# Head 0's gate work moved ahead of the samples' projection, and the samples' state updates moved behind their products

## The chip, the cores and the metric

One core of one Trainium2 chip runs the kernel. The metric is the device time of one execution in microseconds (us); the time before is the median of three runs. The engines are named as in the profile: PE (matrix products), DVE (vector), ACT (scalar, activations and copies), POOL (elementwise work and 16-bit splits), SP (its queue issues most DMAs).

## The reference

One inference step of a two-layer decoder: a gated linear attention (GLA) layer, then a differential-attention layer, each followed by a squared-ReLU MLP, all with a layer norm behind the residual. The model width is 1024. There are 1024 prompt tokens in one sequence, 16 learned tokens ahead of them, and 8 running samples of one token each, which carry a GLA state and a paged cache of 4096 positions. What the change touches is the GLA layer:

```python
q, k, v, r, g_low = split(x @ w_in)            # 4 heads, q and k 128 wide, v and r 256 wide
lg = log_sigmoid(g_low @ w_gate + b_gate) / 16 # a decay for every token and key element
# per head: S_t = diag(exp(lg_t)) S_{t-1} + k_t^T v_t ;  o_t = q_t S_t
b = cumsum(lg);  scores_ij = sum_d q_id k_jd exp(b_id - b_jd), j <= i
o = q exp(b) S + scores v ;  S' = exp(b_last) S + (k exp(b_last - b))^T v
out = (rms_norm(o) * silu(r)) @ w_out
```

The samples do the same with one token each from a loaded state of 4 heads x 128 x 256 (0.5 MB a sample), and write the updated state back. Everything is float32.

## The kernel before, in words

The prompt's work and the samples' work lie side by side in one program. A scheduler fixes, before anything runs, one order of instructions for each engine; on the chip each engine takes its own list in that order and waits at an instruction until its inputs and buffers are ready. So an instruction that waits holds everything behind it on its engine.

**Prompt.** The 1024 tokens lie transposed in two halves of 512 (c = 0, 1), split into a high and a low part (XH, XL). A product in float32 is three matmuls (`mm3`, L206 to L208: high x high, high x low, low x high). Weights come as 256 KB pieces through a raw buffer (L191), ACT casts the high part (L193), POOL makes the low part (L194). `proj(h)` (L304 to L332) is a generator: it makes q and k of head h (4 pieces of 24 matmuls, 512 wide), then v (4 pieces of 48 matmuls, 256 wide), which go into the wide buffer Y. The head loop (L633 to L712) runs for each of 4 heads: the gate (L640, `log_gate` L390 to L395), a running sum (`scan`, L648), seven levels of decays (`level`, L427 to L433, with block products L658 and L673 and masked copies L667), the transposes of k (L693), and the advance of the state over 8 tiles (L701 to L705), whose outputs go back into Y (L708, L709), with a norm on POOL at the end of a head (L712). Behind the loop comes the projection of r, whose Silu is kept in a tile of the same pool as the samples' weights.

**Samples.** The 32 rows (16 learned tokens, 8 samples) go through the same weights in plain float32, from 1 MB tiles (`swt`, a pool of two buffers): the projection (L354 to L366), the gates and the learned tokens' state SM (L400 to L458), the learned tokens' own scores sA (L461 to L473), then a loop over the 8 samples (L482 to L494). For each sample it loads the state into one of three slots of Y (L487), loads the sample's v row broadcast over the partitions (L488, `vs`, into one half of a `swt` tile), multiplies state by q on PE into one accumulator (L490), multiplies the v row by k on POOL (L491), updates the state with four DVE instructions (L493) and writes it out (L494). Behind it come the output's norm (`so`, L508; `soT`, L515 and L516), the product with w_out (`s_rows`, L520 to L526), the residual norm (`s_post`, `s_ln`, L529 to L570), the MLP (L578 to L588, with 16 tiles of w1 and 16 of w2) and the projection of the second layer (L594 to L599 and once more `s_rows`; 12 tiles).

In the program's text the whole of the samples' work stands ahead of the head loop; only 8 of head 0's projection pieces are put into it by hand (`next(first)`). The order on the engines mixes the two.

Of the kernel before, what the change touches and what calls it, by code (L numbers as in the profile page):

```python
# [11 lines left out]
F32 = mybir.dt.float32  # L12
# [9 lines left out]
P = 128  # L22
D = 1024
# [91 lines left out]
def hybrid_step(ctx, tc, A, dbg=None, upto=9):  # L115
# [158 lines left out]
    dma(graw, wir[:, :, 3072:3088])  # L274
    for c in range(2):
# [65 lines left out]
    for c in range(2):  # L341
# [6 lines left out]
        V.tensor_tensor(go, go, ga, op=ALU.add)  # L348
    qk = {}
    first = proj(0, qk)  # L350
    next(first)
# [3 lines left out]
    for k in range(NB):  # L355
# [3 lines left out]
        if k % 2:  # L359
            next(first)  # L360
    for k in range(0, NB, 2):
# [21 lines left out]
    wg = gp.tile([48, 512], F32, name="wg")  # L383
    for c in range(2):
        dma(wg[32 * c : 32 * c + 16, :], A["gla_w_gate"][0])

    def log_gate(z, n, h):

        a = t2()[:, :n]
        S.activation(a, z, AF.Abs, bias=bg[:, h : h + 1])  # L390
        S.activation(a, a, AF.Exp, scale=-1.0)
        S.activation(a, a, AF.Ln, bias=1.0)
        m = t2()[:, :n]
        V.tensor_scalar(m, z, bg[:, h : h + 1], 0.0, ALU.add, ALU.min)
        V.tensor_tensor(m, m, a, op=ALU.subtract)  # L395
        return m

# [24 lines left out]
    def level(b, q, k, u, s, eng):  # L422

        sh = [P, b.shape[1] // (2 * s), 2 * s]
        bv = b.rearrange("p (n s) -> p n s", s=2 * s)
        uv = u.rearrange("p (n s) -> p n s", s=2 * s)
        V.tensor_tensor(uv, bv, bv[:, :, s - 1 : s].broadcast_to(sh), op=ALU.subtract)  # L427
        S.activation(uv[:, :, :s], uv[:, :, :s], AF.Exp, scale=-1.0 / 16)
        S.activation(uv[:, :, s:], uv[:, :, s:], AF.Exp, scale=1.0 / 16)
        kv = k.rearrange("p (n s) -> p n s", s=2 * s)  # L430
        qv = q.rearrange("p (n s) -> p n s", s=2 * s)
        eng.tensor_tensor(uv[:, :, :s], uv[:, :, :s], kv[:, :, :s], op=ALU.mult)
        eng.tensor_tensor(uv[:, :, s:], uv[:, :, s:], qv[:, :, s:], op=ALU.mult)  # L433


# [18 lines left out]


# [26 lines left out]
    vbs = swt()  # L482
    for b in range(NS):
        stt = Y[:, 5120 + 1024 * (b % 3) : 6144 + 1024 * (b % 3)].rearrange("p (h e) -> p h e", e=256)
        vb = vbs[:, b % 2, :].rearrange("p (h e) -> p h e", e=256)
        with tc.issue_after(w_in):
            dma(stt, A["state_gla"][0, b].rearrange("h d e -> d h e"))  # L487
# [145 lines left out]
    for h in range(GH):  # L633
        if h:
            for _ in proj(h, qk):
                pass
# [1002 lines left out]
```

## Time and profile before

| | |
|---|---|
| median of three runs | 2850.98 us |
| lowest, highest | 2846.44, 2857.75 us |
| the profiled execution's own time | 2854.69 us |
| its span in the trace | 2852.8 us |
| mean granted TensorE clock | 0.986 |
| PE, DVE, ACT, POOL busy | 2741.8, 1962.4, 1095.6, 1104.5 us |

A row of the profile names the line of the program, the engine, the operation, what it writes and reads with the shape, and behind the brackets how long the engine had stood idle and which instruction or DMA released it. In a table by stage, "PE busy (x)" is the busy time and the number of instructions, and "PEclk" is the clock that the throttle granted, as a share of full speed. The part of the program that the change touches lies between about 40 and 430 us of the span; the second layer and both prompt MLPs lie behind.

### The profile page before, as it was taken

What the parts mean: (1) busy time and instruction counts of PE and PEld (TensorE: products, weight loads), DVE (VectorE), ACT (ScalarE), POOL (GpSimd) and SP (SyncE); (2) the same over time, 40 slices, a digit from 0 to 9 for tenths busy, and PEclk for the clock granted to TensorE, in tenths of its full rate; (3) what the DMA queues carried; (4) which work ended last, traced back from release to release, by engine and by line L of the source; (5) the groups of instructions that cost most, each with busy time, mean ns of one, the idle gap of its engine ahead of it and who ended that gap; (6) DMA issues with size and microseconds to landing.
All of it is one profiled execution on the core that took longest, in us unless ns stands there. A gap on an engine that the chain in (4) does not pass through costs nothing.

```text
span 2852.8 us, 52251 instructions
## 1 busy us (share of the span) xinstructions
PE 2741.8 (96%) x19849; PEld 2247.6 (79%) x19849; DVE 1962.4 (69%) x3045; ACT 1095.6 (38%) x2230; POOL 1104.5 (39%) x744
## 2 busy tenths in 40 slices
PE   8889999999999999999999999899999999999997
PEld 5676677997777777777798989677898889797985
DVE  2565454658887887677667740887648878878788
ACT  3233344242221321221242112777535546355553
POOL 1221212233443443444333322200026767667764
PEclk9899999999999999999999999999999999999999
DMA  7557751634798898979748995222144555555584
GB/s 246 181 178 259 262 177 33 238 105 150 259 344 306 313 352 297 362 288 327 256 158 302 366 365 173 61 62 70 38 120 88 116 128 117 132 119 115 130 190 87
DMA packets 270968, 561.23 MB, mean 197 GB/s; under 512 B 23462, under 2 KB 138732, under 8 KB 266620
## 3 DMA queue, kind: packets, MB, share of 16 engines
q1 hardware_dynamic: 251420, 521.18, 52.9%
q0 software_dynamic: 19296, 36.71, 7.9%
q8 instruction: 156, 2.56, 0.4%
q14 instruction: 96, 0.79, 0.1%
HBM read 531.42 MB, written 29.52 MB: 197 GB/s over the span
## 4 chain that ended last, share of the span: by engine, by line
PE 72%; DVE 10%; DMA 7%; issue 4%; ACT 4%; POOL 2%; SPq 0%; DVEq 0%; POOLq 0%; ACTq 0%
PE mmt L206 17%; PE mmt L207 17%; PE mmt L208 17%; PE smt L852 4%; PE axt L206 3%; PE axt L207 3%; PE axt L208 3%; PE smt L1223 2%; ACT as L1201 1%; DMA swt<-in_mlp_w 1%; PE prt L1197 1%; DVE Y L1555 1%; DVE RX L1459 1%; DMA rw<-in_mlp_w 1%; DMA pg<-in_cache_k 1%
## 5 line engine op out<-in xcount | busy, mean ns | idle before, releaser
L194 POOL TENSOR_TENSOR wlo<-raw,whi 128x512 fp32r<-128x512 f32 x256 | 371.8, 1466 | 737.4 <-ACT whi L193 656.5
L206 PE MATMUL mmt<-whi,XH 128*128 128x256 f32 (+1 forms) x1760 | 524.5, 300 | 4.2 <-ACT Y L330 3.0
L207 PE MATMUL mmt<-wlo,XH 128*128 128x256 f32 (+1 forms) x1760 | 524.5, 299 | 1.3 <-POOL wlo L194 1.3
L206 PE MATMUL mmt<-XH,whi 128*128 128x512 f32 (+1 forms) x1216 | 436.9, 360 | 6.9 <-DVE Y L922 3.0
L208 PE MATMUL mmt<-whi,XL 128*128 128x256 f32 x1536 | 434.4, 286 | 0.0
L208 PE MATMUL mmt<-XH,wlo 128*128 128x512 f32 (+1 forms) x1216 | 432.6, 356 | 0.0
L193 ACT CAST whi<-raw 128x512 fp32r<-128x512 f32 x256 | 152.8, 619 | 570.6 <-PE mmt L208 186.6
L206 PEld LDWEIGHTS mmt<-whi,XH 128*128 128x128 f32 x1760 | 332.2, 189 | 27.6 <-issue 10.6
L812 DVE TENSOR_REDUCE sc<-pg 128x16 f32<-128x1024 f32 x256 | 308.3, 1212 | 65.9 <-POOL pg L811 63.4
L207 PEld LDWEIGHTS mmt<-wlo,XH 128*128 128x128 f32 x1760 | 333.6, 190 | 24.9 <-issue 12.6
L811 DVE TENSOR_TENSOR pg<-pg,qb 128x1024 f32<-128x1024 f32 x192 | 266.3, 1394 | 59.4 <-DMA pg<-in_cache_k 51.7
L207 PE MATMUL mmt<-XL,whi 128*128 128x512 f32 x768 | 306.4, 399 | 0.0
L208 PEld LDWEIGHTS mmt<-whi,XL 128*128 128x128 f32 x1536 | 289.6, 190 | 5.5 <-issue 4.6
L206 PEld LDWEIGHTS mmt<-XH,whi 128*128 128x128 f32 x1216 | 230.3, 190 | 54.2 <-issue 12.9
L811 POOL TENSOR_TENSOR pg<-pg,qb 128x1024 f32<-128x1024 f32 x64 | 161.3, 2522 | 259.1 <-DMA pg<-in_cache_k 187.6
L208 PEld LDWEIGHTS mmt<-XH,wlo 128*128 128x128 f32 x1216 | 230.4, 190 | 34.6 <-issue 2.1
L206 PE MATMUL mmt<-whi,HH 128*128 128x512 f32 x512 | 204.8, 401 | 4.1 <-DVE Y L1036 3.7
L208 PE MATMUL mmt<-whi,HL 128*128 128x512 f32 x512 | 204.0, 398 | 0.0
L207 PE MATMUL mmt<-wlo,HH 128*128 128x512 f32 x512 | 203.5, 397 | 0.0
L1484 POOL TENSOR_TENSOR wlo<-RW,whi 128x512 fp32r<-128x512 f32 x96 | 169.7, 1807 | 55.7 <-ACT whi L1483 55.7
L1484 POOL TENSOR_TENSOR wlo<-rw,whi 128x512 fp32r<-128x512 f32 x92 | 154.2, 1727 | 80.5 <-ACT whi L1483 78.7
L207 PEld LDWEIGHTS mmt<-XL,whi 128*128 128x128 f32 x768 | 145.2, 189 | 38.2 <-issue 7.1
(424 smaller groups left out, 5716.3 us busy)
## 6 DMA issues: line engine op xcount, KB each, us to landing
pg<-in_cache_k SPq DMA_DIRECT2D x256, 512.0 KB
pg<-in_cache_v SPq DMA_DIRECT2D x256, 512.0 KB
raw<-in_mlp_w SPq DMA_DIRECT2D x164, 256.0 KB
swt<-in_mlp_w SPq DMA_DIRECT2D x32, 1024.0 KB
rw<-in_mlp_w SPq DMA_DIRECT2D x116, 256.0 KB
RW<-in_mlp_w POOLq DMA_DIRECT2D x96, 256.0 KB, 5.7
raw<-in_gla_w_in SPq DMA_DIRECT2D x48, 256.0 KB
swt<-in_gla_w_in SPq DMA_DIRECT2D x12, 1024.0 KB
```

Source lines behind the costliest of these rows:

```text
L193: S.copy(hi[:, c], raw)
L194: G.tensor_tensor(lo[:, c], raw, hi[:, c].bitcast(F32), op=ALU.subtract)
L206: TE.matmul(ps, ah, bh, start=first, stop=False)
L207: TE.matmul(ps, ah, bl, start=False, stop=False)
L208: return TE.matmul(ps, al, bh, start=False, stop=last)
L811: eng.tensor_tensor(pg, pg, qb, op=ALU.mult)
L812: return V.tensor_reduce(sc[:, n, :], pg.rearrange("p (h d) -> p h d", d=64), op=ALU.add, axis=AX.X).ins
L852: m = TE.matmul(acc[i * TS : i * TS + 16, :256], w[r, n, :], pg[r, i * 256 : (i + 1) * 256], start=n == 0, stop=n == NPG).ins
L1197: TE.matmul(pss[m], qs[i][r, ts_], ks[j][r, x:y], start=i + j == 0, stop=i == 1)
L1201: S.activation(sc_[:, m, :W], sc_[:, m, :W], AF.Exp, bias=mns[:, m : m + 1], scale=-1.0, accum_out=l[:, m : m + 1])
L1223: TE.matmul(out, at, v, start=j == 0, stop=j == t + 1)
L1484: G.tensor_tensor(lo[:, k, :], t, hi[:, k, :].bitcast(F32), op=ALU.subtract)
```

## The change

1. `wg` is loaded earlier. The functions `rstd_of`, `log_gate` and `level` are moved ahead, and the body of the head loop is split into `gate_in`, `decays`, `advance` and `head_end`; for heads 1 to 3 they are called as the body was.
2. For head 0, two pieces of the projection (q and k of half 0) are made, then the decays of half 0 (`early(0)`), all in the text ahead of the samples' projection; `early(1)` stands inside it behind its fourth tile. Their results qh and kt are kept in Y[2048:4096].
3. Head 0's `advance` and `head_end` stand right behind SM.
4. The samples' states have five slots, three in Y (5120 and up, as before) and two in a new tile `st2`. The loop over the samples only loads a state and makes its four products. The updates are a function of their own, `state_updates`, which the text calls behind the product with w_out and its norm. It takes samples 5, 6, 7, 3, 4 from the slots in which they lie and loads 0, 1 and 2 a second time (three more loads of 0.5 MB).
5. The broadcast v row lies in Y[4096:5120] and Y[5120:6144] by turns, no longer in a `swt` tile. Y[4096:5120] holds the samples' own v (`sv`) before; Y[5120:6144] is slot 0, so the v row of the second update can be loaded only when the first update's state (slot 0) has been written out.

```diff
+    first = proj(0, qk)
+    for _ in range(2):
+        next(first)
+    early(0)                      # decays(0, 0, gate_in(0, 0), (Y[...2048], ...))
     pa, pb = smt(), smt()
...
         if k % 2:
             next(first)
+        if k == 3:
+            early(1)
...
+    st = SM[:, 0, :]
+    for c in range(2):
+        st = advance(0, c, st, *parts[c])
+    head_end(0, st)
+
...
-    vbs = swt()
+    st2 = spool.tile([P, 2, 1024], F32, name="st2")
+    def slot(i):
+        t = Y[:, 5120 + 1024 * i : 6144 + 1024 * i] if i < 3 else st2[:, i - 3, :]
+        return t.rearrange("p (h e) -> p h e", e=256)
...
     for b in range(NS):
+        state_in(b, b % 5)
         for h in range(GH):
-            TE.matmul(po[...], qmk[:, h, b, :], stt[:, h, :], start=False, stop=b == NS - 1)
-        G.tensor_tensor(vb, vb, bc(skT[:, :, NM + b], [P, GH, 256], 2), op=ALU.mult)
-        for h in range(GH):
-            V.scalar_tensor_tensor(stt[:, h, :], stt[:, h, :], ses[:, h, b : b + 1], vb[:, h, :], ALU.mult, ALU.add)
-        dma(A["gla_state_s"][0, b].rearrange("h d e -> d h e"), stt)
+            TE.matmul(po[...], qmk[:, h, b, :], slot(b % 5)[:, h, :], start=False, stop=b == NS - 1)
+
+    def state_updates():
+        for n, (b, i) in enumerate(((5, 0), (6, 1), (7, 2), (3, 3), (4, 4), (0, 3), (1, 4), (2, 3))):
+            stt = slot(i)
+            if b < 3:
+                state_in(b, i)
+            vb = Y[:, 4096 + 1024 * (n % 2) : 5120 + 1024 * (n % 2)].rearrange("p (h e) -> p h e", e=256)
+            dma(vb.rearrange("p h e -> p (h e)"), A["vs"][b : b + 1, :].broadcast_to([P, D]))
+            G.tensor_tensor(vb, vb, bc(skT[:, :, NM + b], [P, GH, 256], 2), op=ALU.mult)
+            for h in range(GH):
+                V.scalar_tensor_tensor(stt[:, h, :], stt[:, h, :], ses[:, h, b : b + 1], vb[:, h, :], ALU.mult, ALU.add)
+            dma(A["gla_state_s"][0, b].rearrange("h d e -> d h e"), stt)
...
     s_post(s_rows(soT, A["gla_w_out"][0], NB), 0, spool)
+    state_updates()
...
-    for h in range(GH):
-        if h:
-            for _ in proj(h, qk):
-                pass
+    for h in range(1, GH):
+        for _ in proj(h, qk):
+            pass
```

**What stands where, DVE at the samples' output.** Line numbers of the changed kernel differ: its state update is L618, its `so` L626, its `soT` L634, its head state `gS` L462. DVE before, around the copy of the output `so`:

```order
L667 COPY_PREDICATED gAd<-masks,axt 128x128 x2
L681 COPY At_114<-gAd 32x4x32 x4
L493 SCALAR_TENSOR_TENSOR Y<-Y,ses,swt 128x256 x8
L394 TENSOR_SCALAR t_1682<-axt,bg 128x512
L395 TENSOR_TENSOR t_1682<-t_1682,t_1678 128x512
L493 SCALAR_TENSOR_TENSOR Y<-Y,ses,swt 128x256 x4
L648 SCALAR_TENSOR_TENSOR gb<-ones,t_1682 128x128 x4
L705 SCALAR_TENSOR_TENSOR gS<-SM,geb,axt 128x256
L508 COPY so<-smt 128x256
...
L493 SCALAR_TENSOR_TENSOR Y<-Y,ses,swt 128x256 x4
L499 TENSOR_SCALAR rstd<-ssq 128x1
```

Behind these stand the last four updates and the rest of the output's norm. DVE in the changed kernel, at the same copy:

```order
L462 SCALAR_TENSOR_TENSOR gS<-gS,geb,axt 128x256 x3
L618 SCALAR_TENSOR_TENSOR Y<-Y,ses 128x256 x4
L462 SCALAR_TENSOR_TENSOR gS<-gS,geb,axt 128x256
L626 COPY so<-smt 128x256
L356 TENSOR_SCALAR rstd<-ssq 128x1
L629 SCALAR_TENSOR_TENSOR so<-so,rstd,sr 128x256
L462 SCALAR_TENSOR_TENSOR gS<-gS,geb,axt 128x256
L356 TENSOR_SCALAR rstd<-gss 128x8
L618 SCALAR_TENSOR_TENSOR Y<-Y,ses 128x256
L634 COPY soT<-smt 128x2x4x32
L618 SCALAR_TENSOR_TENSOR Y<-Y,ses 128x256 x7
L618 SCALAR_TENSOR_TENSOR st_1399<-st_1399,ses,Y 128x256 x4
```

Before, 28 of the 32 update instructions stand ahead of `so` and the last four directly behind it. Now four (the first sample's) stand ahead of `so`, one (of the second sample) between `so` and `soT`, and eleven between `soT` and the gate of head 1 (the row `t_2270<-axt,bg`, a few rows on). The other sixteen stand further behind.

**The same place on SP**, which issues the loads. Before, the states, the v rows and the states' outputs in turn, with one tile of w_out ahead of most of them and three behind:

```order
L487 DMA Y<-in_state_gla 128x4x256 x3
L488 DMA swt<-vs 128x1024 x2
L240 DMA swt<-in_gla_w_out 128x2x1024
...
L494 DMA out_gla_state_s<-Y 128x4x256
L488 DMA swt<-vs 128x1024
L487 DMA Y<-in_state_gla 128x4x256 x2
L494 DMA out_gla_state_s<-Y 128x4x256
L488 DMA swt<-vs 128x1024
...
L494 DMA out_gla_state_s<-Y 128x4x256
L240 DMA swt<-in_gla_w_out 128x2x1024
L191 DMA raw<-in_gla_w_in 128x2x256
L240 DMA swt<-in_gla_w_out 128x2x1024 x2
```

In the changed kernel two tiles of w_out are issued ahead of these rows, the other two among the first updates' v rows and outputs:

```order
L615 DMA Y<-vs 128x1024
L601 DMA Y<-in_state_gla 128x4x256 x3
L619 DMA out_gla_state_s<-Y 128x4x256
L615 DMA Y<-vs 128x1024 x2
L470 DMA out_gla_state_p<-gS 128x256
L619 DMA out_gla_state_s<-Y 128x4x256
L615 DMA Y<-vs 128x1024
L619 DMA out_gla_state_s<-Y 128x4x256
L240 DMA swt<-in_gla_w_out 128x2x1024
L615 DMA Y<-vs 128x1024
L240 DMA swt<-in_gla_w_out 128x2x1024
L619 DMA out_gla_state_s<-st_1399 128x4x256
```

Each v row (L615) waits on SP until its place in Y is free, and each output (L619) until its update is done. The third and fourth tiles of w_out now stand behind such rows.

**PE at the samples' projection of the second layer**, head 3 of the prompt beside it. Before, between two tiles (L526), pieces of the projection of r stand (L206 to L208 into `mmt`) as well as the head's own block products (L658):

```order
L658 MATMUL axt<-t_3981 32x32 x7
L526 MATMUL smt<-swt,sx 32x512 x4
L658 MATMUL axt<-t_3981 32x32 x9
L658 MATMUL axt<-t_4005 32x32 x16
L526 MATMUL smt<-swt,sx 32x512 x4
L206 MATMUL mmt<-XH_86,whi 128x512
L207 MATMUL mmt<-XL_89,whi 128x512
L208 MATMUL mmt<-XH_86,wlo 128x512
L206 MATMUL mmt<-XH_87,whi 128x512
L207 MATMUL mmt<-XL_89,whi 128x512
L208 MATMUL mmt<-XH_87,wlo 128x512
```

In the changed kernel (tiles: L718 for q and k, L644 for v) only the head's block products (L410, L425) and its advance (L458 to L460) stand between the tiles:

```order
L410 MATMUL axt<-gq,gk 32x32 x16
L718 MATMUL smt<-swt,sx 32x512 x4
L459 MATMUL axt<-gS,t_4104 128x256
L460 MATMUL axt<-Y,t_4116 128x256
L425 MATMUL axt<-t_4183 32x64 x8
L425 MATMUL axt<-t_4199 32x32 x8
L644 MATMUL smt<-swt,sx 32x512 x4
L410 MATMUL axt<-t_4216 32x32 x16
L644 MATMUL smt<-swt,sx 32x512 x4
L410 MATMUL axt<-t_4240 32x32 x16
L410 MATMUL axt<-t_4264 32x32 x16
```

The projection of r begins ahead of these rows, among the first tiles, and goes on behind the third L644 tile. In both kernels a piece of r is emptied from its PSUM bank (a pool of three) by its Silu, which writes into a tile of the pool `swt`, behind all tiles of the samples' weights.

More of the change, by code (lines that the diff above doesn't have):

```diff
@@ L274, in hybrid_step @@
     dma(graw, wir[:, :, 3072:3088])
+    wg = gp.tile([48, 512], F32, name="wg")
+    for c in range(2):
+        dma(wg[32 * c : 32 * c + 16, :], A["gla_w_gate"][0])
     for c in range(2):
@@ L715, in hybrid_step @@
+            st = advance(h, c, st, *decays(h, c, pgs[c]))
+        head_end(h, st)
     fmv = Y.rearrange("p (h c m t) -> p h c m t", h=GH, c=2, m=2)
```

218 lines of the change are left out of this document (112 added, 106 removed).

## The prediction

> **What bounds the kernel now.** The first view is the page's list of busy times: PE works in 96% of the span, and none of the other engines comes near.
>
> ```profile
> span 2852.8 us, 52251 instructions
> PE 2741.8 (96%) x19849; PEld 2247.6 (79%) x19849; DVE 1962.4 (69%) x3045; ACT 1095.6 (38%) x2230; POOL 1104.5 (39%) x744
> ```
>
> The change leaves PE's matmuls as they are, so it can win only time in which PE stands idle or runs at a lower clock. The table by stage, over the part that the change touches, says where that is (the first pair of numbers is PE's, PEclk is the granted clock):
>
> ```profile
> 40.00:110.00 70.00, 70.00 (x508) 52.95 (x509) 9.52 (x27) 14.97 (x35) 15.35 (x11) 1.00 0.68 228
> 110.00:190.00 80.00, 58.89 (x751) 43.99 (x753) 60.78 (x137) 29.43 (x81) 19.45 (x11) 0.81 0.59 191
> 214.00:373.00 159.00, 149.12 (x1750) 107.80 (x1742) 87.17 (x189) 60.53 (x160) 30.25 (x17) 0.99 0.69 237
> 373.00:422.00 49.00, 45.91 (x453) 30.65 (x451) 21.11 (x43) 21.13 (x48) 11.19 (x6) 1.00 0.69 242
> 422.00:640.00 218.00, 215.58 (x1609) 192.27 (x1608) 119.29 (x194) 88.14 (x157) 65.21 (x44) 1.00 0.36 121
> ```
>
> From 110 to 190 us, where head 0's gate work and the samples' states meet, PE is idle for 80 - 58.89 = 21.1 us, and its 58.89 us ran at a clock of 0.81, which loses 0.19 x 58.89 = 11.2 us. That is **32.3 us of loss**, and the pool from which the change can draw. 40 to 110 has none, 214 to 373 has 9.9 us (the samples' MLP weights), 373 to 422 has 3.1 us (the samples' last projection).
>
> The timeline of PE names the waits inside that stage, and the chain of waits the states' loop:
>
> ```profile
> 127.40 1.49 PE L673 MATMUL axt<-t 128*32 128x64 f32 x32 [5.65 <-DVE t L433]
> 135.02 1.08 PE L490 MATMUL smt<-Y,s 128*32 128x256 f32 x8 [2.86 <-DMA Y<-in_state_gla]
> 151.60 0.64 PE L490 MATMUL smt<-Y,s 128*32 128x256 f32 x8 [3.16 <-DMA Y<-in_state_gla]
> 167.59 0.58 PE L206 MATMUL mmt<-whi,XH 128*128 128x256 f32 x1 [3.02 <-ACT Y L330]
> ```
>
> ```profile
> 140.72 5.71 DMA out_gla_state_s<-Y
> 146.44 0.37 SPq L487
> 146.91 0.46 SPq L494
> 147.46 6.64 DMA swt<-vs
> 154.29 1.88 POOL swt L491
> 156.19 3.71 DVE Y L493 x4
> 178.83 4.97 DMA swt<-in_gla_w_out
> ```
>
> PE waits for head 0's levels on DVE (5.65 us), for states whose slot must first be updated and written out (2.86, 3.16), and for a cast queued on ACT behind the level work (3.02). The change takes away the first two by what it does: the gate work gets a place under the projection, and the products no longer stand behind the updates of three slots.
>
> **The change part by part.** The stage's 32.3 us go, and in their place come these losses.
>
> (a) *Head 0's decays between projection pieces.* They issue about 60 DVE instructions a half. DVE is empty there, and PE is busy throughout:
>
> ```profile
> 40.00:90.00 50.00, 50.00 (x359) 37.42 (x359) 0.00 (x0) 8.57 (x15) 6.38 (x5) 1.00 0.81 275
> 120.41 3.10 DVE L427 TENSOR_TENSOR t<-gb 128x512 f32<-128x512 f32 x5
> 212.34 2.42 DVE L648 TENSOR_TENSOR_SCAN gb<-ones,t 128x128 f32<-128x128 f32 x4
> ```
>
> A level costs DVE 3.10 / 5 = 0.62 us for its subtraction and about as much for its two products, so seven levels with the scan (2.42) are near 12 us, and with ACT's turns between some 20 us. PE has 50 us of projection there, so it is hidden, unless PE's queue holds a block product ahead of a projection piece before DVE has got there. I take 1.5 us, between 0 and 9 (DVE's chain met in full twice is the 5.65 of the row above, and again half of it). If the cover failed wholly it would cost those 9 us.
>
> (b) *ACT's casts.* Evictions of v (the 3.02 us) still stand behind casts and exponentials on ACT. I take 2 us, 0 to 4.
>
> (c) *soT behind the second update.* The changed order puts one update instruction of the second sample in front of soT on DVE, and its v row's place is the first sample's slot. So soT, and behind it w_out's matmuls on PE, wait for a chain: the first update, its output DMA, the v row's load, POOL's multiply, the update. The chain's own rows above give 5.71 + 0.9 (two issues) + 6.64 + 1.88 = 15.1 us, and the first update itself is 1.67:
>
> ```profile
> 123.43 1.67 DVE L493 SCALAR_TENSOR_TENSOR Y<-Y,ses,swt 128x256 f32<-128x256 f32 x4
> 80.00:84.00 4.00, 4.00 (x36) 4.00 (x35) 0.00 (x0) 0.00 (x0) 0.00 (x0) 1.00 0.91 328
> 147.35 0.59 PE L702 MATMUL axt<-SM,t 128*128 128x256 f32 x2
> ```
>
> That is 16.8 us from the product of sample 5 to the row ahead of soT. Between that product and w_out PE has 69 matmuls of 256 columns at 4.00 / 36 = 0.111 us (7.7 us), three products at 0.64 (1.9; L490's row) and six matmuls of the advance's and transposes' kind at some 0.35 (2.1; from 0.59 for an overlapping pair): 11.7 us. PE is idle for about 5.1 us. Behind an idle time of this kind the clock falls, as the stage shows around the wait that ended at 167.59:
>
> ```profile
> 166.00:169.00 3.00, 1.41 (x6) 1.41 (x7) 3.00 (x10) 1.54 (x4) 1.55 (x1) 0.65 0.47 159
> 169.00:172.00 3.00, 3.00 (x15) 2.94 (x14) 2.19 (x4) 0.76 (x3) 1.91 (x2) 0.50 1.01 284
> ```
>
> 0.35 x 1.41 + 0.50 x 3.00 = 2.0 us lost by the clock. I take 7 us, between 4 (the transfers a quarter shorter) and 12 (they collide with w_out's tiles, 4.97 each). The Trainium skill, "TensorE: Matmul & The Clock Gate", section "Part 1: The HAM clock gate", has the clock halved after an idle window of about 3.4 us and given back after about 3.4 us of work: by it the clock's part would be an estimated 1.7 us, and the sum 0.3 us lower. The trace differs in that 3.02 us of idle time were enough.
>
> (d) *w_out's third and fourth tile* now stand on SP behind the first updates' outputs and v rows, where SP waits for the updates. Behind SP's waits hang only these tiles, and PE's w_out for them. I take 2 us, between 0 and 5 (a tile's 4.97).
>
> (e) *The first norm beside updates on DVE.* Seven and four update instructions stand between soT and head 1's gate, at 1.67 for four. What of them meets the norm's short DVE steps delays w1's first product: 2 us, 0 to 5 (11 x 0.42 = 4.6). Three more loads of 0.5 MB ride on SP in this stage; they and the remaining sixteen updates have the MLP's 159 us, in which DVE is idle for 72: nothing. If that cover is gone, the four rows of an update come to stand in the path of head 1's levels, 1.67 each (rival C).
>
> (f) *The MLP's weights*, 214 to 373: as now, 9.9 us.
>
> (g) *The last projection of the samples.* Its twelve 1 MB tiles have two buffers. Now PE has pieces of the projection of r between them and is the slower side. In the changed order only three pieces of r can precede (their Silu needs a `swt` buffer), so less work lies between the tiles. From the second tile to the twelfth PE has 38 matmuls of 512 columns, ten tiles, eleven sets of block products and some 14 advance matmuls:
>
> ```profile
> 101.00:110.00 9.00, 9.00 (x40) 7.33 (x40) 3.99 (x19) 3.25 (x14) 1.93 (x2) 1.00 0.23 59
> 415.06 1.06 PE L526 MATMUL smt<-swt,sx 128*32 128x512 f32 x8 [1.59 <-DMA swt<-in_diff_w_in]
> 131.50 0.66 PE L658 MATMUL axt<-t 128*32 128x32 f32 x32 [1.32 <-DVE gAd L667]
> ```
>
> 38 x 9.00 / 40 = 8.6, ten at 1.06 = 10.6, eleven at 0.66 = 7.3, 14 at 0.35 = 4.9: 31 us. The ten tiles and about four raw pieces of 256 KB are 11.5 MB, and where DMA set the pace it moved 275 GB/s (40 to 90): 42 us. So PE is idle for 11 us, where it has 3.1 now: **+8 us**. At 242 GB/s (the same place now) the tiles take 47.5, +13; at 328 (80 to 84) 35, +1.
>
> Sum: 1.5 + 2 + 7 + 2 + 2 = 14.5 us in place of 32.3, and 8 given back at the tail: a gain of 32.3 - 14.5 - 8 = 9.8 us. The profiled execution took 2854.69 us (its span 2852.8 and what lies around it), so this one would take 2844.9. It stood 3.7 us above the median of the runs; the median I forecast is **2841 us**. 0.5% is 14 us, about what a measurement of this kernel can tell from no change: 2837 and 2865 are the bounds.
>
> **The rivals.**
>
> A, *the whole pool is won.* (c) falls to 4, (d) and (e) to 0, (a) and (b) to 1 and 0, and the tail gives back 2, since a tile may run at 328 GB/s. Gain 32.3 - 5 - 2 = 25 us: 2854.69 - 25 - 3.7 = 2826. For it speaks that each wait named above is removed by the order itself; against it, the new chain in (c), each link of which has its row.
>
> B, *the tail becomes the bound, and the kernel is slower.* Two tiles that do not overlap take what the last two of now took, one behind the other:
>
> ```profile
> 407.83 7.19 DMA swt<-in_diff_w_in
> 415.08 5.48 DMA swt<-in_diff_w_in
> ```
>
> A pair in 12.7 us is 63.5 us for ten tiles; against 31 us of work PE is idle for 32, +29 over now, and with the clock at 0.50 (169 to 172) over some 12 us of the work another 6. The gain turns into 32.3 - 14.5 - 35 = -17: 2868. It decides against the change once the tail gives back over 17.8 us, and beyond 0.5% from 32 on. Against it: from 373 to 422 the same twelve tiles, PE-paced, came in 49 us.
>
> C, *POOL slows DVE's updates and levels.* The update with a POOL row beside it took 3.71 us where it takes 1.67 alone, and now eight v-row multiplies and eight updates lie beside head 1's levels:
>
> ```profile
> 156.11 2.71 POOL L194 TENSOR_TENSOR wlo<-raw,whi 128x512 fp32r<-128x512 f32 x2
> ```
>
> Four updates at 2 us more are 8 us on the path of head 1's gate: gain 2, 2849. The Trainium skill, "GPSIMD Engine Reference", section "1. Specifications", says that GpSimd's SBUF interfaces are shared with VectorE, in contention with DVE instructions of two SBUF inputs; the trace agrees in this one row.
>
> Also possible is that the change does not do what its words say: 16 of 32 updates still stand ahead of head 1's gate on DVE, five ahead of soT. That is (c) and (e), in the forecast.
>
> **How the numbers follow.** Forecast 0.40, A 0.38, B 0.12, C 0.10. The forecast's own range, by its terms' bounds taken two at a time, is 2833 to 2852. To hold the time 8 times in 10 the range takes in A with its spread and C: 2820 to 2862, and leaves out most of B. Faster by over 0.5%: A, and the lucky end of the forecast, less A's weak end: 0.40. Slower: B and a little of C: 0.14. Same: 0.46.
>
> **What would show it.** In the profile of the changed kernel: PE with no idle time of over 2 us between 40 and 110 (a); the waits of PE for states and for head 0's levels gone; one wait of 4 to 8 us ahead of w_out, released by soT on DVE, and in the chain the output DMA, a v row and POOL's multiply before it (c); waits of PE for `in_diff_w_in` of about 11 us together at the samples' last projection (g); and from there on a table as now (215.58 busy of 218). I am wrong if the idle time ahead of w_out is over 12 us, if the tail loses under 2 or over 18, or if PE loses over 10 us in head 0's decays.

## The result, and the profile after

The changed kernel takes **2834.48 us** (median of 8 runs, 2827.53 to 2839.16) against 2847.49 us for the kernel before (8 runs, 2846.10 to 2857.75): a ratio of 0.9948, 95% interval [0.9936, 0.9960]. That is 13.0 us less; the forecast was 9.8 less. A second comparison, among the experiments below, gave 0.9957 [0.9942, 0.9972].

The two profiled executions stand 24 us apart in their spans (2852.8 and 2828.8), more than the medians. A mark that both programs share tells how much of it belongs to the change: the first addition of the prompt's first MLP on DVE. These are its rows, of before and then of the changed kernel (shortest, median and longest duration in ns, then the first and last start):

```profile
L1036 DVE TENSOR_TENSOR Y<-Y,mmt x128: 634/678/692, 672.4 to 1447.1; 128x512 f32<-128x512 f32 x128
```

```profile
L1081 DVE TENSOR_TENSOR Y<-Y,mmt x128: 632/678/689, 655.8 to 1429.7; 128x512 f32<-128x512 f32 x128
```

The changed kernel is 16.6 us ahead there and 17.4 at the last of these rows. The other 7 us came up further on, where the programs do the same; single executions of one kernel differ by that much (before: 2846 to 2858).

The table by stage of the changed kernel, over the stretches of the prediction (its 110 to 214 covers two of them):

```profile
0.00:40.00 40.00, 27.79 (x128) 18.22 (x129) 16.74 (x35) 16.20 (x28) 9.69 (x12) 0.91 0.75 249
40.00:110.00 70.00, 69.84 (x888) 52.16 (x887) 35.71 (x85) 28.29 (x66) 8.81 (x7) 1.00 0.58 200
110.00:214.00 104.00, 98.64 (x782) 76.03 (x781) 55.37 (x129) 32.12 (x95) 36.19 (x20) 0.95 0.58 189
214.00:373.00 159.00, 152.52 (x1645) 110.68 (x1644) 77.26 (x177) 61.23 (x161) 36.83 (x21) 0.99 0.72 247
373.00:422.00 49.00, 40.88 (x601) 25.91 (x600) 33.13 (x84) 21.89 (x59) 1.61 (x1) 0.97 0.67 232
422.00:640.00 218.00, 216.94 (x1385) 193.96 (x1383) 110.40 (x159) 76.51 (x130) 67.81 (x46) 1.00 0.40 129
```

And the first stretch of before, which the prediction did not show:

```profile
0.00:40.00 40.00, 29.76 (x141) 20.07 (x145) 16.65 (x35) 15.95 (x28) 9.16 (x11) 0.96 0.76 252
```

PE's loss is its idle time and what the clock took from its busy time. From 110 to 214 it was 32.3 us and is 104 - 98.64 + 0.05 x 98.64 = 10.3. From 40 to 110, where DVE now has 85 instructions in place of 27, it is still nothing: the gate work is hidden whole. At the end of the samples' path (373 to 422) it rose from 3.1 to 8.1 + 0.03 x 40.88 = 9.3. PE's remaining waits, from its timeline:

```profile
182.29 1.94 PE L644 MATMUL smt<-swt,soT 128*32 128x512 f32 x8 [3.77 <-DMA swt<-in_gla_w_out]
206.31 0.41 PE L669 MATMUL smt<-ss,c_inv 128*128 128x32 f32 x2 [1.59 <-DVE ss L667]
410.20 1.06 PE L644 MATMUL smt<-swt,sx 128*32 128x512 f32 x8 [2.37 <-DMA swt<-in_diff_w_in]
415.88 0.79 PE L206 MATMUL mmt<-XH,whi 128*128 128x512 f32 x1 [1.53 <-ACT swt L774]
```

The waits for head 0's levels, for states and for ACT's cast are gone. One wait of size is new, 3.77 us at w_out; it is released by the third weight tile, not by soT. The chain that the prediction feared ahead of soT (the first update, its output DMA, a v row into the slot that it leaves, POOL's multiply, the update row) isn't what held soT. These rows of DVE, SP, POOL and PE show what ran:

```profile
157.64 1.67 DVE L618 SCALAR_TENSOR_TENSOR Y<-Y,ses 128x256 f32<-128x256 f32 x4 [1.26 <-PE smt L606]
...
167.09 0.48 DVE L618 SCALAR_TENSOR_TENSOR Y<-Y,ses 128x256 f32<-128x256 f32 x1
167.49 0.42 DVE L634 COPY soT<-smt 128x256 f32<-128x256 f32 x1
```

```profile
159.34 0.38 SPq L619 DMA_DIRECT2D out_gla_state_s<-Y  x1
159.82 0.45 SPq L615 DMA_DIRECT2D Y<-vs  x1
163.57 0.33 SPq L615 DMA_DIRECT2D Y<-vs  x1
...
172.78 0.61 SPq L240 DMA_DIRECT2D swt<-in_gla_w_out  x1
```

```profile
165.15 1.91 POOL L616 TENSOR_TENSOR Y<-Y,sqk 128x1024 f32<-128x1024 f32 x1 [2.66 <-DMA Y<-vs]
168.03 2.03 POOL L616 TENSOR_TENSOR Y<-Y,sqk 128x1024 f32<-128x1024 f32 x1 [0.98 <-DMA Y<-vs]
```

```profile
156.92 0.64 PE L606 MATMUL smt<-Y,s 128*32 128x256 f32 x8
...
169.31 1.92 PE L644 MATMUL smt<-swt,soT 128*32 128x512 f32 x16
```

Two v rows were issued here. SP waited 3.2 us for the output DMA before the second of them (163.57), and not before the first (159.82). By the semaphores of the trace the first landed at 165.02 and the second at 167.97; POOL's multiply at 165.15 and the DVE row at 167.09 waited for the first. The same semaphores tie that DVE row to the state that was loaded third, sample 7. So the row ahead of soT belongs to sample 7, the third in the text, whose v row lies in Y[4096:5120] and needs only that the first update is done. The v row that goes into slot 0, behind the output, is sample 6's, and its update stands behind soT.

From the first update to sample 7's row it took 167.09 - 157.64 = 9.45 us, and PE had work from the end of sample 5's product (156.92 + 0.64) to w_out at 169.31, 11.8 us, without a gap.

### The profile page after: what moved, and what is told of

Read it like the earlier page. It is cut to its first block, busy times and chain, and to the rows that moved or that the text cites. A ratio compares the mean times of both kernels' runs of the same rounds, so it can differ in the third digit from the quotient of the medians.

```text
span 2828.8 us, 52247 instructions
## 1 busy us (share of the span) xinstructions
PE 2735.8 (97%) x19849; PEld 2242.1 (79%) x19849; DVE 1937.3 (68%) x3045; ACT 1084.4 (38%) x2221; POOL 1115.2 (39%) x744
## 5 line engine op out<-in xcount | busy, mean ns | idle before, releaser
L194 POOL TENSOR_TENSOR wlo<-raw,whi 128x512 fp32r<-128x512 f32 x256 | 379.1, 1495 | 727.2 <-ACT whi L193 589.2
L206 PE MATMUL mmt<-whi,XH 128*128 128x256 f32 (+1 forms) x1760 | 523.1, 300 | 1.3 <-DVE ast L1244 0.9
L206 PE MATMUL mmt<-XH,whi 128*128 128x512 f32 (+1 forms) x1216 | 435.3, 359 | 6.8 <-DVE Y L967 3.0
L208 PE MATMUL mmt<-whi,XL 128*128 128x256 f32 x1536 | 433.1, 285 | 0.0
L208 PE MATMUL mmt<-XH,wlo 128*128 128x512 f32 (+1 forms) x1216 | 432.5, 356 | 0.0
L207 PEld LDWEIGHTS mmt<-wlo,XH 128*128 128x128 f32 x1760 | 332.5, 189 | 24.8 <-issue 11.8
L206 PEld LDWEIGHTS mmt<-whi,XH 128*128 128x128 f32 x1760 | 330.8, 189 | 24.6 <-issue 11.8
L208 PEld LDWEIGHTS mmt<-whi,XL 128*128 128x128 f32 x1536 | 288.8, 189 | 6.5 <-issue 5.8
L206 PEld LDWEIGHTS mmt<-XH,whi 128*128 128x128 f32 x1216 | 230.0, 189 | 49.4 <-issue 7.6
L208 PEld LDWEIGHTS mmt<-XH,wlo 128*128 128x128 f32 x1216 | 230.0, 189 | 36.6 <-issue 4.1
L206 PE MATMUL mmt<-whi,HH 128*128 128x512 f32 x512 | 204.7, 401 | 3.9 <-DVE Y L1081 3.6
L208 PE MATMUL mmt<-whi,HL 128*128 128x512 f32 x512 | 203.9, 398 | 0.0
```

What stands on the lines that cost most here:

```text
L194: G.tensor_tensor(lo[:, c], raw, hi[:, c].bitcast(F32), op=ALU.subtract)
L206: TE.matmul(ps, ah, bh, start=first, stop=False)
L207: TE.matmul(ps, ah, bl, start=False, stop=False)
L208: return TE.matmul(ps, al, bh, start=False, stop=last)
```

## The experiments

Each kernel was timed in five rounds beside the kernel before. The table gathers them. The loss of PE is taken from each kernel's table by stage: the stretch less PE's busy time times its granted clock, added over the rows of the stretch.

| kernel | ratio to before [95%] | loss 110-220 | 220-380 | 380-520 | first w1 product | last tile's product |
|---|---|---|---|---|---|---|
| before | 1 | 32.7 | 11.4 | 4.6 | 213.8 | 421.1 |
| changed | 0.9948 [0.9936, 0.9960] | 10.3 | 8.0 | 9.7 | 218.2 | 423.3 |
| changed, again | 0.9957 [0.9942, 0.9972] | 10.4 | 10.6 | 9.1 | 219.9 | 426.3 |
| early gate alone | 1.0048 [1.0029, 1.0066] | 8.6 | 8.4 | 33.0 | 245.1 | 454.4 |
| states alone | 1.0008 [0.9998, 1.0019] | 21.3 | 13.4 | 6.0 | 191.2 | 398.1 |
| early gate, Silu's own buffer | 0.9975 [0.9962, 0.9989] | 8.6 | 4.7 | 10.5 | 240.8 | 451.3 |
| changed, Silu's own buffer | 0.9925 [0.9912, 0.9938] | 10.3 | 10.0 | 4.0 | 218.9 | 429.8 |
| changed, updates behind w_out | 0.9986 [0.9975, 0.9998] | 13.0 | 9.7 | 15.4 | 225.6 | 442.8 |
| changed, updates in the MLP | 0.9991 [0.9974, 1.0009] | 3.7 | 32.6 | 9.9 | 212.3 | 444.1 |
| the same, Silu's own buffer | 0.9983 [0.9969, 0.9997] | 1.9 | 28.4 | 9.9 | 210.7 | 451.0 |
| changed, no updates | 0.9904 [0.9890, 0.9917] | 2.7 | 8.7 | 4.8 | 210.2 | 409.0 |
| before, three weight buffers | 1.0005 [0.9992, 1.0018] | 32.0 | 7.8 | 5.6 | 198.3 | 365.9 |
| changed, three weight buffers | 0.9924 [0.9908, 0.9939] | 7.4 | 8.2 | 0.3 | 230.2 | 390.1 |
| the same, Silu's own tiles | 0.9934 [0.9921, 0.9947] | 11.0 | 7.1 | 2.0 | 229.7 | 391.8 |

One profiled execution stands behind each row of losses, and it can lie well off its kernel's median: 9 us under it for the early gate with the Silu's own buffer, 9 us over it for the updates in the MLP. So the losses say where the time goes, and the ratio how much it is. Differences from the changed kernel are taken below from 0.9948; from its second ratio, 0.9957, a gain would be 2.6 us larger.

### Either half alone

My theory was that the early gate and the split states each win a part. The first kernel keeps the early gate and takes back the loop of before:

```diff
-        state_in(b, b % 5)
+        with tc.issue_after(w_in):
+            dma(stt, A["state_gla"][0, b].rearrange("h d e -> d h e"))
+        dma(vb.rearrange("p h e -> p (h e)"), A["vs"][b : b + 1, :].broadcast_to([P, D]))
         for h in range(GH):
             TE.matmul(...)
+        G.tensor_tensor(vb, vb, ...)
+        for h in range(GH):
+            V.scalar_tensor_tensor(stt[:, h, :], ...)
+        dma(A["gla_state_s"][0, b].rearrange("h d e -> d h e"), stt)
...
-    state_updates()
```

> Only the first half of the change: head 0's gate work and advance stand early, but the samples' states are loaded, multiplied, updated and written in one loop with three slots, as before. My theory: both halves of the change share the gain, since in the profile of before PE waited 7.2 us for states and 5.65 + 1.3 us for head 0's levels, and the lost clock (11.2 us) belongs to both. Then this kernel keeps the waits for states and gains about half of the change: 5 to 9 us under before, and PE waits of 5 us or more for in_state_gla are in its profile. The rival: the gate's place is all that counts, and states that wait for their slot are hidden once DVE is free of head 0's levels. Then it is as fast as the changed kernel, 12 to 15 us under before, and the waits for in_state_gla are under 2 us.

It was **slower** than before by 0.48% (2863.3 us, 2848.82 beside it). The stage from 110 to 220 did get better, 8.6 us of loss in place of 32.7, but the samples' path came later: sample products from 151 to 186 us (before 119 to 158), first w1 product at 245. The loss reappears at the end of that path. The table by stage and three of PE's waits in it:

```profile
380.00:440.00 60.00, 42.71 (x503) 23.64 (x503) 28.59 (x81) 17.34 (x54) 5.24 (x2) 0.84 0.53 180
440.00:520.00 80.00, 76.43 (x347) 58.74 (x348) 16.17 (x23) 22.13 (x37) 15.40 (x12) 0.93 0.24 71
```

```profile
427.79 1.06 PE L703 MATMUL smt<-swt,sx 128*32 128x512 f32 x8 [1.58 <-DMA swt<-in_diff_w_in]
430.77 1.67 PE L703 MATMUL smt<-swt,sx 128*32 128x512 f32 x8 [1.92 <-DMA swt<-in_diff_w_in]
434.01 1.93 PE L703 MATMUL smt<-swt,sx 128*32 128x512 f32 x8 [1.56 <-DMA swt<-in_diff_w_in]
```

Tile after tile PE waits for the next one, with no prompt work left beside it, and 60 - 42.71 x 0.84 + 80 - 76.43 x 0.93 = 33 us are lost. Both theories were wrong: the early gate alone gives nothing, and its states' loop is no longer what PE waits for most (2.3 us for in_state_gla in all).

The second kernel keeps the five slots and leaves head 0's gate in the head loop:

```diff
-    for _ in range(2):
-        next(first)
-    early(0)
+    next(first)
...
-        if k == 3:
-            early(1)
...
-    for h in range(1, GH):
-        for _ in proj(h, qk):
-            pass
+    for h in range(GH):
+        if h:
+            for _ in proj(h, qk):
+                pass
```

> Only the second half: five slots, products first, updates behind w_out in the text; head 0's gate work stays in the head loop, as before. My theory: PE still waits for head 0's levels (5.65 us before, and the clock lost behind it), but no longer for states: 4 to 8 us under before. The rival by which the gate's place is all: 0 to 2 us under before. A third way: DVE, which has head 0's levels to do but no updates ahead of so, reaches the levels sooner, and this half alone gives nearly everything, over 10 us.

No difference (2851.86 us): the rival by which the gate's place is all fits the number, but not the reason. The samples' path did gain, its first w1 product at 191.2 us in place of 213.8. PE's rows say where that went:

```profile
110.00:160.00 50.00, 38.29 (x421) 27.06 (x419) 36.95 (x89) 18.42 (x51) 14.25 (x7) 0.83 0.52 174
300.00:380.00 80.00, 71.71 (x835) 52.11 (x834) 45.19 (x102) 31.14 (x80) 14.33 (x8) 0.98 0.57 197
```

```profile
352.98 0.70 PE L459 MATMUL axt<-gS,t 128*128 128x256 f32 x2 [2.76 <-DVE gS L462]
```

Head 0's levels still leave PE 50 - 38.29 x 0.83 = 18.2 us short, and from 300 to 380 a head's advance waits for DVE in a stretch where the samples' tiles filled in before (9.7 us of loss, 5.5 before). So each half shifts the samples' path, by 20 to 30 us one way and the other, and the two shifts cancel: with both, w1 begins at 218.2, near where it was, and head 0's gate is out of the way. The gain belongs to the pair. What brought the path of the early gate alone to its late place is the order in which the scheduler put the pieces; that was read from the traces and not tried apart.

### The end of the samples' path

If the end of that path is what the early gate pays with, work let in beside its tiles must give it back. The Silu of r gets another tile, so pieces of r can be emptied early:

```diff
-        silt = swt().rearrange("p k (c n) -> p k c n", c=2)
+        silt = (swt() if h % 2 else st2).rearrange("p k (c n) -> p k c n", c=2)
```

> The changed kernel, but the Silu of r for heads 0 and 2 writes into the second state tile, which is free by then, and not into the samples' weight pool, so that pieces of the projection of r can be emptied ahead of the samples' last weight tiles and stand between them on PE. My theory: the 8.1 us that PE is idle from 373 to 422 us in the changed kernel come from too little work between the twelve tiles, so they fall to 3 us or less and the kernel is 4 to 6 us faster than the changed one. The rival: the matmuls between the tiles are the same work moved, and the idle time returns at the end of the projection of r, where the last transposes wait for DVE and ACT: within 2 us of the changed kernel.

On the changed kernel it made 2826.86 us, ratio 0.9925: 6.5 us better than the changed kernel's 0.9948. The loss from 380 to 520 fell from 9.7 to 4.0, as the theory had it. The same edit on the early gate alone:

> The early gate alone (states in one loop, as before), with the Silu of r for heads 0 and 2 in a buffer of its own. The early gate alone was 13.7 us slower than before, and its profile has the samples' last tiles from 411 to 455 us (373 to 421 in before), with some 20 us of idle time and a clock of 0.71 to 0.78 there. My theory: the early gate pushes the samples' path 30 us later, and that costs at the end, where the tiles have no other work of PE left beside them; with the pieces of r let in, this kernel is 12 to 20 us faster than the early gate alone, so equal to before or a little under it. The rival: the early gate alone is slow for its states' loop, in which soT comes 54 us behind the first product; then the buffer for r gives back less than 6 us.

2843.61 us, ratio 0.9975, in place of 1.0048: 0.73%, or 21 us, given back, with the states' loop untouched. The row at that place, to be held against 42.71 at 0.84 above:

```profile
380.00:440.00 60.00, 53.72 (x515) 36.57 (x514) 32.00 (x78) 27.69 (x64) 9.25 (x6) 0.97 0.49 172
```

That is rival B's mechanism: the place, the tiles without work beside them, and a price of 21 us. In the changed kernel it was there at some 6 us.

The changed kernel once more, on the chip of the kernels that follow:

> The changed kernel once more, unaltered, beside the next three on one chip. All theories: 10 to 17 us under before, and the same stages in its profile: about 4 us of waiting for w_out's third tile, and about 8 us of idle time of PE around the samples' last projection.

2837.88 us beside 2848.58, ratio 0.9957.

### The updates' place

w_out's third tile was issued at 172.78 us and its product began at 182.29. I took the updates' transfers for the cause and put them behind:

```diff
+        w_last = swl[-1]
...
-            dma(vb.rearrange("p h e -> p (h e)"), A["vs"][b : b + 1, :].broadcast_to([P, D]))
+            with tc.issue_after(w_last):
+                dma(vb.rearrange("p h e -> p (h e)"), A["vs"][b : b + 1, :].broadcast_to([P, D]))
```

> The changed kernel, but the v rows of the updates are loaded only once w_out's last tile has been issued, so that the updates are all behind soT on DVE and behind w_out's tiles on SP. In the profile of the changed kernel PE waits 3.77 us for w_out's third tile, which was issued 2.5 us after its buffer came free and took 9.5 us to land beside the updates' transfers, and the clock falls behind that wait. My theory: the updates' transfers are the cause, so this wait falls under 1.5 us and the kernel is 3 to 5 us faster than the changed one. The rival: the tile is late because only two buffers exist, and a tile needs 5 us or more on any path: the wait stays over 2.5 us and the time is within 2 us of the changed kernel. It could lose if the updates now press on the MLP's tiles: then waits for in_mlp_w grow by what is won here.

The wait at w_out did go, and w_out's last product began at 182.4 us in place of 191.9; but the kernel made 2846.92 us, ratio 0.9986, and lost most of the change's gain. w1 began at 225.6, later than in the changed kernel. Its DVE timeline shows a step of the first norm (L669) among the updates (L620) and behind head 1's levels, and the levels themselves slowed:

```profile
190.10 7.01 DVE L376 TENSOR_TENSOR t<-gb 128x512 f32<-128x512 f32 x5
...
202.85 1.66 DVE L620 SCALAR_TENSOR_TENSOR Y<-Y,ses 128x256 f32<-128x256 f32 x4
204.43 0.59 DVE L669 TENSOR_REDUCE ss<-sz 128x32 f32<-128x256 f32 x1
204.94 1.66 DVE L620 SCALAR_TENSOR_TENSOR Y<-Y,ses 128x256 f32<-128x256 f32 x4
```

```profile
190.90 3.36 POOL L194 TENSOR_TENSOR wlo<-raw,whi 128x512 fp32r<-128x512 f32 x2 [4.71 <-ACT whi L193]
194.22 2.35 POOL L618 TENSOR_TENSOR Y<-Y,sqk 128x1024 f32<-128x1024 f32 x1
```

PE waits 4.1 us there for these levels and 2.9 us for the norm. The subtractions of five levels took 7.01 us beside POOL's work; in before they took 3.10 us, at 120.41, where POOL stood idle. The Trainium skill, "GPSIMD Engine Reference", section "1. Specifications", has the two engines share their SBUF interfaces; these rows agree, though they don't tell how much of the 3.9 us is that. So the cause that I named was there and was not what mattered: the updates' place in the changed kernel, between the samples' output and its norm, is better than this one.

Then further back, beside the MLP, where DVE looked free:

```diff
     for half in range(2):
...
+            if half == 0 and k == 5:
+                state_updates(w1_in)          # v rows issued after this tile's load
```

> The changed kernel, but the v rows of the updates are loaded only once the sixth tile of the MLP's w1 has been issued, so the updates stand behind w_out and behind its norm, in a stretch in which DVE is busy for 3 to 7 us of 20 in the changed kernel. With the updates just behind w_out's tiles the kernel lost 12 us of the changed kernel's gain, though w_out ended 9.5 us sooner: the norm took 43 us from w_out to w1 where it takes 26 in the changed kernel. My theory: the updates lay in front of the norm's short steps and head 1's levels on DVE; behind the norm they cost neither, so w_out's wait is under 1.5 us, the norm takes under 26 us, and the kernel is 4 to 8 us faster than the changed one. The rival: the updates cost 13 us of DVE and 8 of POOL wherever they stand, and they now meet heads 1 and 2 and the MLP's tiles: within 3 us of the changed kernel, or slower.

> Both: updates behind the sixth tile of w1, and the Silu of r for heads 0 and 2 in the second state tile. If the two gains are separate, it is faster than the changed kernel by their sum: 6.5 us from the Silu's buffer (as that kernel measured) and 4 to 8 from the updates, so 2818 to 2825. If the samples' path ends earlier by the updates' move, the end has less to gain from the buffer, and it is no faster than the better of the two alone.

2848.01 us (0.9991) and 2844.66 us (0.9983). The stage ahead is now nearly free of loss (3.7 us), and the MLP pays for it:

```profile
220.00:300.00 80.00, 59.68 (x726) 41.59 (x724) 55.92 (x111) 27.00 (x77) 23.38 (x12) 0.83 0.85 296
```

```profile
274.79 1.94 PE L705 MATMUL smt<-swt,sx 128*32 128x512 f32 x8 [4.34 <-DMA swt<-in_mlp_w]
282.90 1.49 PE L425 MATMUL axt<-t 128*32 128x64 f32 x32 [6.17 <-DVE t L382]
```

80 - 59.68 x 0.83 = 30.5 us of loss. The updates' v rows, outputs and reloads are 8 x 0.5 + 8 x 0.5 + 3 x 0.5 = 9.5 MB, which meet the MLP's own tiles on DMA, and a head's levels on DVE. My theory failed; the rival that they cost wherever they stand fits. The Silu's buffer gave 0.08% there, inside the intervals, since the loss was elsewhere.

What they cost in the changed kernel was measured by leaving them out:

```diff
-            vb = Y[...]
-            dma(vb.rearrange("p h e -> p (h e)"), A["vs"][b : b + 1, :].broadcast_to([P, D]))
-            G.tensor_tensor(vb, vb, ...)
-            for h in range(GH):
-                V.scalar_tensor_tensor(stt[:, h, :], ...)
             dma(A["gla_state_s"][0, b].rearrange("h d e -> d h e"), stt)
```

> The changed kernel without the updates: no v rows, no POOL multiplies, no state updates on DVE. The eight states are still loaded (three of them twice) and written out, but not updated, so the samples' state output is the input. It bounds what the updates cost in the changed kernel. My theory: they cost what the trace shows around them, w_out's wait of 3.8 us with its half clock (about 2 us) and 1 to 2 us at the norm, so 6 to 10 us are gained on the changed kernel. The rival: their 13 us of DVE and 8 of POOL are hidden, and the wait at w_out is for the state transfers, which are still there: 0 to 3 us gained.

2824.0 us, ratio 0.9904 against 0.9948: 0.44%, 12.5 us, more than the 6 to 10 expected. In the profiled execution 7.6 us of it lie from 110 to 220, where w1 begins 8 us sooner; 4.9 lie at the end of the samples' path, whose last tile comes 14 us sooner. The second part was missing from my expectation. (Its figure for POOL was too low as well: eight multiplies at 1.91 us are 15 us.)

### A third weight buffer

All of PE's waits for tiles could be a matter of two buffers. In the kernel before there is room for a third (one number changed):

```diff
-    swp = p1.enter_context(tc.tile_pool(name="swp", bufs=2))
+    swp = p1.enter_context(tc.tile_pool(name="swp", bufs=3))
```

> The kernel before with a third buffer for the samples' 1 MB weight tiles, nothing else. In before PE waits for these tiles 1.1 us at w_out, 6.4 us in the MLP and 3.1 us at the last projection, some 10 us; the 32 us of loss between 110 and 190 us are head 0's levels and the states. My theory: the buffer takes at most those 10 us, so 4 to 10 us under before, and the loss from 110 to 190 us stays. The rival: PE's idle time in the tiles' stretches is not set by the buffers but by DMA, and nothing is won (within 3 us). A third: the buffer alone gives what the whole change gives (12 us or more).

Nothing was won, where my theory had 4 us at least: 2848.80 beside 2848.39 us, although the samples' path ended 55 us sooner (last product at 365.9). The 32 us from 110 to 220 are untouched, and PE's work does not shrink because the samples' part of it comes early.

In the changed kernel the third buffer needs the room of the second state tile:

```diff
-    st2 = spool.tile([P, 2, 1024], F32, name="st2")
+    vb2 = s4()
...
-        state_in(b, b % 5)
+        state_in(b, b % 3)
...
-((5, 0), (6, 1), (7, 2), (3, 3), (4, 4), (0, 3), (1, 4), (2, 3))
+((5, 2), (6, 0), (7, 1), (0, 2), (1, 0), (2, 1), (3, 2), (4, 0))
...
-            if b < 3:
+            if b < 5:
-            vb = Y[:, 4096 + 1024 * (n % 2) : 5120 + 1024 * (n % 2)]...
+            vb = (vb2 if n % 2 else Y[:, 4096:5120])...
```

> The changed kernel with three buffers for the weight tiles. To make room the states have three slots again (no second state tile): products first, then samples 5, 6 and 7 are updated where they lie and the other five are loaded a second time (five reloads where the changed kernel has three); the second v row lies in the buffer of the products' masked q, not in slot 0. My theory: w_out's third tile is then there when soT is (3.8 us of waiting and the clock behind it gone), and the tail's idle time (8 us) halves: 4 to 9 us faster than the changed kernel. The rival: the two more reloads and the transfers, all moved forward by a third buffer, press on the first norm and on head 1's levels as they did in the two kernels that moved the updates: no faster than the changed kernel.

2826.61 us, ratio 0.9924: 0.24%, 6.8 us, better than the changed kernel, and the end of the samples' path is free of loss:

```profile
380.00:440.00 60.00, 59.73 (x666) 45.60 (x666) 34.48 (x79) 43.32 (x83) 10.64 (x8) 1.00 0.23 72
```

At w_out PE now waits 3.35 us for soT, so that part of the expectation is wrong. Here the four rows of one update stand ahead of soT on DVE, and they take 7.67 us beside POOL's work, where the four of the first update take 1.67. Together with tiles of its own for the Silu (SM and `s4()` for heads 0 and 2):

> The kernel with three weight buffers, and besides the Silu of r for heads 0 and 2 in two small tiles that are free by then, not in the weight pool. My theory: a third buffer and pieces of r beside the tiles both serve the tail, so they do not add up: between 0 and 4 us faster than three buffers alone, and the fastest kernel of all if three buffers alone is faster than the changed one. The rival: they add up, 6 us or more.

2828.05 us, 0.9934: not to be told from three buffers alone. They do not add up; either one takes away most of the loss at the end. Each of the three kernels with one of them or both is under the kernel before by 0.66% or more, and under the changed kernel by 0.14 to 0.24%. Their intervals overlap with its own ([0.9936, 0.9960]), so these last gains are likely and not certain.

## Why the prediction came out as it did, point by point

- **The pool.** Right: the stage's 32.3 us were what could be won. 10.3 are left there, by the row from 110 to 214; forecast was 14.5.
- **(a), (b).** Forecast 1.5 and 2 us, measured 0.16 and nothing: DVE's 85 instructions from 40 to 110 us lie under the projection, and of PE's waits from 110 to 640 us none is for ACT's evictions of v. The cover was as good as its rows said.
- **(c)** Forecast 7 us with 4 as the least, measured nothing. This is the step that failed. PE's work was sized rightly (11.7 forecast, 11.8 measured), but the chain had a link too many. The update row ahead of soT was taken for the second of the text, whose v row must wait for the first update's output. It is sample 7's, and its v row went out at 159.82, beside that output and not behind it: from the first update's end to sample 7's row it took 167.09 - 159.31 = 7.8 us, of which 0.5 went to the issue, 5.2 to the v row and 1.9 to POOL. By the prediction's own rows the 16.8 us without the output (5.71) and its issue (0.45) are 10.6, less than PE's 11.7 us of work, so nothing would have been forecast. The price of the link was too high as well. Sample 6's chain does go through slot 0; its v row landed at 167.97 and its multiply ended at 170.06. Had its row stood ahead of soT, soT would have been ready at 170.9, and PE idle for about 1.6 us; that is an estimate from these rows, with 0.4 us each for the row and the copy.
- **(d)** Forecast 2 us, at most 5. Measured 3.77 of idle time, and the clock behind it, from these rows:

```profile
182.00:185.00 3.00, 2.71 (x18) 1.23 (x19) 1.84 (x5) 0.00 (x0) 0.98 (x1) 0.50 0.98 366
185.00:188.00 3.00, 3.00 (x11) 2.36 (x10) 2.93 (x6) 0.09 (x1) 0.92 (x1) 0.67 0.97 261
```

  0.50 x 2.71 + 0.33 x 3.00 = 2.3 us more, 6.1 in all. The term had no clock in it. The one wait that the prediction looked for at w_out, released by soT ahead of the first tile, did not come; the one that came stands ahead of the third tile and is released by its DMA.
- **(e)** Forecast 2, measured 1.59 at the norm, and 0.26 x 2.69 + 0.31 x 3.00 = 1.6 by the clock behind it (rows in the last section). What hangs on the updates altogether is more, 12.5 us by the kernel without them, since a later samples' path is paid for once more at its end. No term of the sum carried such a delay on to the end.
- **(f)** Forecast as before; 8.0 us against 11.4 (clock included): 3.4 better.
- **(g)** Forecast +8, measured 9.3 - 3.1 = +6.2. PE's waits for `in_diff_w_in` were 5.6 us together, where the prediction's sign was about 11. The reason given (no pieces of r between the tiles) is shown: with pieces let in, it fell to 4.0 us and the kernel won 6.5 us.
- **Not in the sum:** the first 40 us. PE lost 10.2 + 0.04 x 29.76 = 11.4 us there and loses 12.2 + 0.09 x 27.79 = 14.7. The two early loads of `wg` (2.63 us of SP's queue at 10.97 us) now stand ahead of the small loads for which PE waits (gla_norm: 0.6 us before, 1.8 now). Nearly all traces with the early load show 3 to 5 us there, one does not (the early gate with the Silu's buffer), and it was not tried apart.
- **The sum.** Loss from 0 to 640 us, before and now: 11.4 + 32.3 + 11.4 + 3.1 + 2.4 = 60.6, and 14.7 + 0.2 + 10.3 + 8.0 + 9.3 + 1.1 = 43.6. The difference, 17.0 us, is that of the mark (16.6) in these two executions; the medians differ by 13.0. The forecast of 9.8 was low by (a) to (c), 10 us that did not come, and by (f) and (g), 3 and 2 us better; against it stand 4 more in (d), 3 at the start and 1 in (e). That it came within some 3 us of the medians is in part luck: its largest loss in the stage, (c), had no chain behind it, and the losses that it missed made up for most of that.
- **The rivals.** A (25 us) is near where the kernels with a third buffer or a Silu tile came (22 and 21 us), with 22 to 25 us won from 110 to 220 and nothing given back at the end. It still had (c) at 4, where nothing was measured. B is real, in the early gate alone. C did not decide here; its rows are seen in the kernel with the updates behind w_out, and in the one with three buffers, ahead of soT.
- **"The change takes away the first two by what it does"** was right of the pair, and would have been wrong of either half. I had not seen that the two halves hold each other up; nothing in the sum asked where the samples' path would stand against the prompt's.

## What to carry to other kernels

Where one engine is the bound and two streams of work share it, ask of a moved step not only which wait goes, but where each stream then stands against the other: the one that comes late ends without work beside it, and the one that comes early takes that work away from a later stretch. A third buffer under the samples' path won 55 us of its time and nothing of the kernel's; a buffer at the place where work ran out won 6 to 21 us. And where a predicted wait hangs on which buffer an instruction uses, look up that buffer: the rows of the order name tile and line, not the slot, and the scheduler had taken the third update ahead of the second.

## What the runs showed of the hardware

In the changed kernel PE's clock fell after an idle time of 1.59 us, with small matmuls behind it. That is the longest idle time from 203 to 212 us (most of it ahead of 206, 0.31 us behind), and the granted clock goes to 0.74 and 0.69, though PE was busy for 2.69 and 3.00 of 3 us with 53 and 73 instructions, most of them small:

```profile
203.00:206.00 3.00, 1.72 (x25) 1.05 (x23) 3.00 (x10) 1.54 (x4) 0.00 (x0) 1.00 0.99 332
206.00:209.00 3.00, 2.69 (x53) 1.76 (x53) 3.00 (x9) 0.95 (x2) 0.00 (x0) 0.74 0.08 27
209.00:212.00 3.00, 3.00 (x73) 2.71 (x73) 3.00 (x8) 0.92 (x2) 0.00 (x0) 0.69 0.03 5
```

The Trainium skill, "TensorE: Matmul & The Clock Gate", section "Part 1: The HAM clock gate", names an idle window of about 3.4 us; here one idle time of 1.59 us was enough, with small products behind it. What of it is the idle time and what the small products was not tried. At w_out, too, the clock did not wait for the end of the idle time: PE stood idle from 178.52 to 182.29, and from 180 to 182 the granted share was already 0.54.
